# Letting four attention units lead, with gate products between their blocks, in a one-layer hybrid attention kernel

## The chip, the cores and the metric

The kernel runs on one core of a Trainium2 chip. A core has a matrix engine (TensorE: PE for its matmuls, PEld for loading their stationary operand), VectorE (DVE), ScalarE (ACT), GpSimd (POOL) and SyncE (SP), which here only issues DMAs. Each engine works through its own instructions in order; engines wait for each other by semaphores. SBUF is the memory beside the engines, PSUM the banks that matmuls write, DRAM lies behind the DMA queues. The metric is the device time of one execution in microseconds.

## The reference

One layer of a diffusion backbone: 1024 latent tokens and a prompt of 128 tokens, width 1024, all in float32. Each token is normed and modulated, projected once into queries, keys, values and gates of two mixers, attended in both, and the gated results are projected out and added to the residual.

```python
h = rmsnorm(xs, norm_gain) * (1.0 + scale) + shift
q_a, k_a, v_a, g_a, q_b, k_b, v_b, g_b = split(h @ w_in)      # q, k: RMS norm per head, axial rotary
o_a = global_attn_latent(q_a, k_a, v_a, cache_k_a, cache_v_a)       # 8 heads, 2 key heads: 128 cached + 1024 latent keys
o_b = window_attn_latent(q_b, k_b, v_b, cache_k_b, cache_v_b, sink) # |i - j| <= 128, cached keys, a sink logit
xs = xs + gate * (concat(o_a * silu(g_a), o_b * silu(g_b)) @ w_out)
```

The prompt goes through the same weights and attends to its own 128 keys. Its keys and values are outputs too.

## The kernel before

Tokens are nine tiles of 128 (tile 0 is the prompt, 1 to 8 the latents). For precision nearly every operand is held as a high part, rounded to the matmul's format, and a low part, the rest; a product is two or three matmuls (high x high, high x low, low x high). So most results are copied once by ACT (the high part) and subtracted once by DVE or POOL (the low part).

The order of the work is that of the Python program: `in_order` at its end (L94) ties every instruction to the one before it on its engine. `tick` (L131) advances a counter, `later(n, f)` (L127) puts a piece of work n ticks ahead. The stages:

1. Norm and modulation, gates of mixer A, then queries of A and of B, which go to DRAM (`q_dram`), then keys and values of both mixers (L749 to L838). Keys of A lie in `kha`, `kla` (high, low), of B in `khb`, `klb`; values in `v_hi`, `v_lo`, where `v_hi` has a half for each mixer.
2. Gates of mixer B, `gates(W_GB, ...)` (L301, L839, L1060): 12 pieces, four for each of the token ranges 0:512, 512:768 and 768:1152 (`THIRDS`). A piece is 24 matmuls, then `put_gates` (L286): one Silu on ACT and a store to DRAM. Between their products run the maxima of two A units (`EARLY`, L1047).
3. The main loop (L1262). A unit is one token tile, one mixer and one key head with its four query heads. Units go in the order A, B, A, B (L849), 32 of them, and the prompt's four last. An A unit has nine key blocks, a B unit three or four. Each pass of the loop is a slot and starts one block: `scores` (L1107), and three slots later (`LAG`) `values` (L1134).

In an A block PE makes two score matmuls of 512 columns, ACT the exponential (L1123) and the high part (L1127), POOL the low part (L1131; DVE for one block in nine), PE three value matmuls (L1141 to L1144). The exponential needs each query's maximum: `max_items` (L864) makes 12 matmuls of 384 columns with a DVE maximum each, some slots ahead. A B unit's `weight_items` (L910) make scores of four heads against `khb`, `klb`, a DVE maximum (L942) and an exponential; its blocks are then PE transposes (L1115).

When a unit's last values are done, `inverse`, `gated` and `parts` (L1150 to L1179) follow at 1, 4 and 6 slots: division, the product with the Silu gate, and the split into `ogh` and `ogl`. Nine slots after a B unit's last values, `out_items` (L1199) of this token tile's group (A's and B's parts) are queued: 24 matmuls of 512 columns with `w_out`. The loop takes 2.5 of them in a slot (`OUTRATE`), 3 in an empty one.

`w_out` is split into parts that take the memory of the modulated tokens as these are used up (`load_wo`, `split_wo`, `WO_STEPS`, `WO_LATE`). After the gates, `p1.close()` (L1067) gives the memory of the gate weights to later tiles, and an ACT table with Exp and Ln is loaded (L1069). Loads and most stores stand in SP's queue, in program order.

## Time and profile before

| | before |
|---|---|
| median of 3 runs | 711.63 us (710.87 to 712.46) |
| profiled execution, first to last instruction (span) | 709.6 us |
| median less span | 2.0 us |
| PE busy, share of the span | 691.6 us, 97% |
| DVE, ACT, POOL busy | 469.3, 409.9, 334.2 us |
| dense stages (projections and gates) | from about 17 to 303 us |
| main loop, first score product to last output product | 303.2 to 704.9 us |
| one steady pair of units (A and B) | 23.88 us |
| DRAM read, written | 58.7 MB, 19.2 MB |

The page of a profile gives, in this order: busy time of each engine; the span in 40 slices, a digit for the busy tenths of each; DMA queues; the chain of work that ended last; the costliest groups of instructions (line, engine, operation, output<-inputs, shapes, count | busy us, mean ns of one | idle time of the engine before them and what ended it); DMA issues. Matmuls overlap in the records: one lasts some 390 ns from start to end while the next starts some 230 ns after it. The profiled execution's own time is not given apart from its span; the three runs are other executions.

### The profile page before, as it was taken

Reading aid. Unit: us, or ns where it says so; the run is one execution under the profiler, and the core shown is the slowest. Engines: PE = TensorE matmul, PEld = TensorE weight load, DVE = VectorE, ACT = ScalarE, POOL = GpSimd, SP = SyncE. Lnnn points to the kernel's source line nnn. Section 1 sums busy time; section 2 is a strip of 40 time slices with the busy share of each in tenths; the row PEclk is TensorE's granted clock in tenths of the full one; section 3 lists DMA queues with packets and bytes.
Section 4 is the critical chain, followed back from the end, with each engine's and each line's share of the span. In section 5 each row is a group of like instructions: output and inputs, shape, how many; then the busy total and the mean of one; then the engine's idle time right before and its main releaser. Section 6 shows DMA issues by size and latency. Waiting matters only on the chain. (4 is left out here: it accounts for less than half of the span.)

```text
span 709.6 us, 10604 instructions
## 1 busy us (share of the span) xinstructions
PE 691.6 (97%) x3508; PEld 558.5 (79%) x3508; DVE 469.3 (66%) x1019; ACT 409.9 (58%) x829; POOL 334.2 (47%) x356
## 2 busy tenths in 40 slices
PE   7999999999999999989999999999999999999987
PEld 4778988878787889966788888888888888787865
DVE  4667257967848945647867578666775776675662
ACT  5646412412403431188777887787778777877760
POOL 3547023233213421256756655665576557555660
PEclk9999999999999999999999999999999999999999
DMA  8962283358353116332222121212221221222323
GB/s 316 415 211 102 78 302 74 90 154 263 84 139 104 37 39 215 123 108 57 78 68 85 50 82 53 71 57 75 68 82 38 79 71 50 78 72 70 104 67 121
DMA packets 53560, 78.58 MB, mean 111 GB/s; under 512 B 7096, under 2 KB 25720, under 8 KB 52608
## 3 DMA queue, kind: packets, MB, share of 16 engines
q1 hardware_dynamic: 45328, 65.96, 28.1%
q10 hardware_dynamic: 8176, 11.94, 6.3%
q8 instruction: 28, 0.46, 0.3%
q14 instruction: 28, 0.23, 0.1%
HBM read 58.69 MB, written 19.18 MB: 110 GB/s over the span
## 5 line engine op out<-in xcount | busy, mean ns | idle before, releaser
L1131 POOL TENSOR_TENSOR pl<-pe,ph 128x512 fp32r<-128x512 f32 x130 | 167.7, 1292 | 145.0 <-DVE nm L942 67.5
L882 DVE TENSOR_REDUCE mx<-pmx 128x1 f32<-128x384 f32 x192 | 101.4, 552 | 56.3 <-PE pmx L881 54.8
L1123 ACT ACTIVATE pe<-st 128x512 f32<-128x512 f32 x146 | 86.8, 594 | 28.2 <-PE st L1121 27.4
L1127 ACT CAST ph<-pe 128x512 fp32r<-128x512 f32 x146 | 90.6, 621 | 4.8
L1141 PE MATMUL pv<-ph,v_hi 128*128 128x512 f32 x208 | 82.8, 398 | 2.2 <-DVE spare L1165 2.2
L1144 PE MATMUL pv<-pl,v_hi 128*128 128x512 f32 x208 | 82.4, 396 | 0.0
L1212 PE MATMUL po<-wo,ogh 128*128 128x512 f32 x216 | 72.6, 395 | 0.2 <-DVE yt L1219 0.2
L174 POOL TENSOR_TENSOR rs_q<-ms_q,mhalf 128x8 f32<-128x8 f32 x18 | 34.1, 1896 | 80.9 <-DVE ms_q L172 80.9
L942 DVE CUSTOM_DVE_ANT_0 sn<-sn,mask,nsink 128x512 f32<-128x512 f32 (+1 forms) x64 | 46.4, 724 | 38.0 <-PE sn L939 37.6
L881 PE MATMUL pmx<-kha,qt 128*128 128x384 f32 x192 | 61.2, 363 | 0.4 <-ACT pen L928 0.2
L1120 PE MATMUL st<-qt,kha 128*128 128x512 f32 x144 | 58.2, 404 | 1.9 <-ACT pe L1123 1.1
L1121 PE MATMUL st<-qb,kla 68*128 68x512 f32 x144 | 57.5, 399 | 1.1 <-DVE qb L901 1.1
L1143 PE MATMUL pv<-ph,v_lo 128*64 128x512 f32 x146 | 57.6, 395 | 0.0
L1144 PEld LDWEIGHTS pv<-pl,v_hi 128*128 128x128 f32 x208 | 39.2, 189 | 16.4
L928 ACT ACTIVATE pen<-sn,nm 128x512 f32<-128x512 f32 (+2 forms) x72 | 45.0, 626 | 6.5 <-DVE nm L942 3.1
L1116 ACT CAST ph<-st 128x512 fp32r<-128x512 f32 x62 | 36.4, 587 | 19.9 <-PE st L1115 18.7
L1141 PEld LDWEIGHTS pv<-ph,v_hi 128*128 128x128 f32 x208 | 39.3, 189 | 10.6 <-ACT ogh L1177 2.4
L646 ACT CAST qo0q<-ptq 128x512 fp32r<-128x512 f32 x18 | 10.6, 586 | 60.7 <-PE ptq L643 55.8
L1212 PEld LDWEIGHTS po<-wo,ogh 128*128 128x128 f32 x216 | 40.0, 188 | 6.8 <-DVE yt L1219 0.6
L1117 DVE TENSOR_TENSOR pl<-st,ph 128x512 fp32r<-128x512 f32 x62 | 42.5, 686 | 2.7 <-ACT ph L1116 2.1
L1212 PE MATMUL po<-wo,ogl 128*128 128x512 f32 x108 | 42.6, 394 | 0.0
L881 PEld LDWEIGHTS pmx<-kha,qt 128*128 128x128 f32 x192 | 35.6, 191 | 6.4 <-DVE mx L882 1.3
(213 smaller groups left out, 1699.2 us busy)
## 6 DMA issues: line engine op xcount, KB each, us to landing
qt<-qd SPq DMA_DIRECT2D x36, 256.0 KB, 3.0
wm<-in_w_mod_ss_dram SPq DMA_DIRECT2D x7, 1024.0 KB, 10.0
qd<-qo0q ACTq DMA_DIRECT2D x36, 128.0 KB, 2.4
qd<-qo1q ACTq DMA_DIRECT2D x36, 128.0 KB, 2.4
sgl<-gd SPq DMA_DIRECT2D x36, 128.0 KB, 2.2
out_dram<-yt SPq DMA_DIRECT2D x17, 256.0 KB, 2.0
xn<-in_x_sample_dram SPq DMA_DIRECT2D x8, 512.0 KB, 7.2
wg<-in_w_mod_g_dram SPq DMA_DIRECT2D x4, 1024.0 KB, 8.3
```

Of the source, the lines that this page charges most:

```text
L881: nc.tensor.matmul(pm[:, 0:384], lhs, kha[:, g, 3 * b : 3 * b + 3, :], start=True, stop=True)
L882: nc.vector.tensor_reduce(mx[:, h, b : b + 1], pm[:, 0:384], axis=AX.X, op=ALU.max)
L942: nc.vector.tensor_tensor_reduce(s, s, mask[:, m0 : m0 + n], -1.0, nsink[:, 4 * g + h : 4 * g + h + 1], op0=ALU.add, op1=ALU.min, accum_ou ...
L1120: nc.tensor.matmul(s, kh, qtile[i], start=True, stop=False)
L1121: nc.tensor.matmul(s, kl, qbtile[i], start=False, stop=True)
L1123: nc.scalar.activation(pe, s, AF.Exp)
L1127: nc.scalar.copy(ph, pe)
L1131: nc.gpsimd.tensor_tensor(pl, pe, ph, op=ALU.subtract)
L1141: nc.tensor.matmul(pv, two, ph, start=(b == 0), stop=False)
L1143: nc.tensor.matmul(pv[0:64, :], vl, ph, start=False, stop=False)
L1144: nc.tensor.matmul(pv, two, pl, start=False, stop=last)
L1212: nc.tensor.matmul(po[n], a, wo_parts[KT * n + k][lo], start=(k == KS[0] and p == 0), stop=(k == KS[-1] and p == 2))
```

## The change

- Only the first four pieces of mixer B's gates (tokens 0:512) are made in the dense stage, with the maxima of the first A unit beside the last two. The other eight pieces, 192 matmuls, become a list `light` of single products: 12 units of them (a unit is a product of 512 columns) before the first slot, then 4.2 in each slot (`fill`).
- Their Silu can't be had from the ACT table that the main loop uses. `late_gates` makes it of a DVE maximum, Exp, Ln (of 1 + x), Exp on ACT, and `late_put` of a DVE product, then the store.
- The unit order is A0 A1 A2 A3, then A4 B0 A5 B1 ... A15 B11, then B12 to B15, each behind five empty slots (`GAP`), then the prompt's four. In the tail the output products go at 4 a slot (`OUTTAIL`), and the B units' small steps are closer (`EX_TAIL`, `ROWS_TAIL`).
- An A unit's gated output waits in DRAM (`of_dram`) until its B unit starts: `fetch` loads it there, and three slots later `split_out` makes `ogh` and `ogl`.
- The low parts of B's keys and both parts of B's values go to DRAM as they are made (`klb_dram`, `vb_dram`), and come back in one load each when the gate pieces are done and `p1` is closed (`finished`, three slots after the last product).
- The last parts of `w_out` are loaded and split in other slots (`WO_MID`, `WO_LAST`).

The core of the diff ("..." marks lines left out):

```diff
+LEADERS = 4
+LIGHT = 4.2
+PRE = 6
+GAP = 5
+MX_LEADER = (0, 0, 1, 1, 2, 2, 3, 3, 4, 4, 5, 5)
+LEADER_END = 6
-WO_LATE = {12: 8, 13: 9, 11: 21, 14: 22, 15: 23}
+WO_MID = ((7, 4, 10), (8, 5), (9, 6), (10, 8))
+WO_LAST = ((12, 10, 11), (13, 11, 14), (11, 19, 15), (14, 20), (15, 24))
+EX_TAIL = (1, 1, 3)
+ROWS_TAIL = (1, 1, 3, 4)
+OUTTAIL = 4.0
...
-        gb = gates(W_GB, 1, None, THIRDS)
+        gb = gates(W_GB, 1, None, THIRDS[:1])
...
-    units = [(t, m, g) for t in range(1, NT) for g in range(2) for m in range(2)]
-    units[PROMPT_AT:PROMPT_AT] = [(0, m, g) for g in range(2) for m in range(2)]
+        order = [(t, 0, g) for t in range(1, NT) for g in range(2)]
+        units = order[:LEADERS]
+        for u, (t, m, g) in enumerate(order):
+            if LEADERS + u < len(order):
+                units.append(order[LEADERS + u])
+            units.append((t, 1, g))
+        units += [(0, m, g) for g in range(2) for m in range(2)]
...
+                    lb = kt.tile([P, 2, P], F32R, tag="lb", name=f"lb{nm}")
...
-                            low.append((klb[:, g, 1::3, :], four, khb[:, g, 1::3, :]))
...
+                    low.append((lb, p4[:, 2:4], khb[:, :, at, :]))
+                    def put_low():
+                        for a in (1, 4, 7, 10) if blk == 0 else (at,):
+                            nc.sync.dma_start(klb_dram[:, :, a, :], lb.bitcast(F32))
+                    later(2, put_low)
...
+    def late_gates(pg, ch, ts):
+        n = ts.stop - ts.start
+        sg = wrp.tile([P, 512], F32, tag="raw", name=f"sg1_{ch}_{ts.start}")[:, 0:n]
+        nc.vector.tensor_scalar(sg, pg, -80.0, None, op0=ALU.max)
+        nc.scalar.activation(sg, sg, AF.Exp, scale=-1.0)
+        nc.scalar.activation(sg, sg, AF.Ln, bias=1.0)
+        nc.scalar.activation(sg, sg, AF.Exp, scale=-1.0)
+        later(1, lambda: late_put(pg, sg, ch, ts))
+    def late_put(pg, sg, ch, ts):
+        nc.vector.tensor_tensor(sg, pg, sg, op=ALU.mult)
+        r0 = 512 + P * ch
+        nc.sync.dma_start(g_dram[r0 : r0 + P, ts], sg)
+    for a, b in THIRDS[1:]:
+        for ch in range(4):
+            light += piece_items(ch, slice(a, b), (lambda a=a: marks[a]()) if ch == 3 else None)
...
+    def finished(gate):
+        p1.close()
...
+        nc.sync.dma_start(klb.bitcast(F32), klb_dram)
+        nc.sync.dma_start(vb.bitcast(F32), vb_dram)
...
+        for i in (12, 13):
+            load_wo(i, late_pools["b2"])
+        wo_steps(WO_LAST)
+        for n in range(2):
+            nc.sync.dma_start(gate[n], gate_row[0:1, 512 * n : 512 * n + 512].to_broadcast([P, 512]))
...
+            if m == 0 and t:
+                nc.sync.dma_start(of_dram[t, g], v["of"])
+            else:
+                split_out(t, 2 * m + g, v["of"])
...
+    def fetch(t, g):
+        ofl = areas["spare"][:, 1280:1536].rearrange("p (c n) -> p c n", c=2)
+        nc.sync.dma_start(ofl, of_dram[t, g])
+        later(3, lambda: split_out(t, g, ofl))
...
+        if i >= TAIL and units[i][0]:
+            slots += [None] * GAP
...
+    def fill(n):
+        rate[0] = min(rate[0] + n, 8.0)
+        while light and rate[0] >= light[0][0]:
+            n, f = light.pop(0)
+            rate[0] -= n
+            f()
+    for _ in range(2):
+        fill(PRE)
+        tick()
...
-        for f in due.get(s, ()):
+        for f in due.get(s, ())[:1]:
             f()
-        rate = OUTRATE if s < len(slots) and slots[s] else PADRATE
-        credit = min(credit + rate, 6.0) if outq else 0.0
+        fill(LIGHT / 2)
+        for f in due.get(s, ())[1:]:
+            f()
+        fill(LIGHT / 2)
+        rate_ = OUTTAIL if s >= start[TAIL] - GAP else OUTRATE if s < len(slots) and slots[s] else PADRATE
+        credit = min(credit + rate_, 6.0) if outq else 0.0
```

More of the change, by code (lines that the diff above doesn't have):

```diff
@@ L33 @@
 WRAW = 3
-PROMPT_AT = 32
 KS = (0, 1, 4, 5, 2, 3, 6, 7)
@@ L1044, in hybrid_step @@
     later(2, lambda: nc.vector.tensor_copy(mask, mask32))
[L1045 to L1054 removed]
+    u_load(2)
     for i in range(4):
         load_wo(i)
[L1058 to L1059 removed]
@@ L1088, in blocks @@
         p0, p1_ = window(t)
         at = {p: b + 1 for b, p in enumerate(POS)}
-        return [(p - p0, v_hi[:, 1, 2 * at.get(p, 0) + g], None) for p in range(p0, p1_)]
+        return [(p - p0, 2 * at.get(p, 0) + g) for p in range(p0, p1_)]
     pvb, og = {}, {}
```

349 lines of the change are left out of this document (195 added, 154 removed).

## The prediction

> **What bounds the kernel now.** I read the page's busy table and slices first, then the busy time of each engine stage by stage, then the waits inside the stages that are not full. The page:
>
> ```profile
> span 709.6 us, 10604 instructions
> PE 691.6 (97%) x3508; PEld 558.5 (79%) x3508; DVE 469.3 (66%) x1019; ACT 409.9 (58%) x829; POOL 334.2 (47%) x356
> ACT  5646412412403431188777887787778777877760
> PEclk9999999999999999999999999999999999999999
> ```
>
> TensorE (PE) is the bound, at full clock, and the change neither adds nor removes a matmul. So the time can change only by the idle time of PE that it closes or opens, and by the pace of products that get other neighbours. The stages (columns: length, then busy us with the count of instructions for PE, weight load, DVE, ACT, POOL, then clock and DMA). The first two rows are the gate products of mixer B (dense stage); the next four and the last two are cut where a unit of mixer A begins its first scores:
>
> ```profile
> 272.00:284.00 12.00, 12.00 (x98) 12.00 (x97) 9.87 (x20) 1.15 (x3) 2.58 (x2) 1.00 0.65 200
> 284.20:303.10 18.90, 18.90 (x111) 18.74 (x110) 13.07 (x28) 1.86 (x4) 3.88 (x3) 1.00 0.37 122
> 303.18:321.90 18.72, 15.86 (x74) 10.90 (x72) 8.74 (x20) 16.83 (x35) 10.45 (x10) 1.00 0.34 98
> 321.90:341.64 19.74, 18.94 (x87) 13.93 (x88) 14.21 (x34) 16.28 (x35) 15.19 (x16) 1.00 0.26 78
> 341.64:367.12 25.48, 24.84 (x120) 19.77 (x119) 18.66 (x38) 19.67 (x39) 16.56 (x17) 1.00 0.26 77
> 390.96:414.84 23.88, 23.88 (x116) 19.24 (x116) 15.26 (x34) 18.73 (x38) 14.10 (x15) 1.00 0.21 64
> 650.53:673.66 23.13, 22.64 (x115) 18.21 (x114) 14.07 (x28) 18.67 (x44) 14.17 (x16) 1.00 0.36 118
> 673.66:704.88 31.22, 29.25 (x132) 22.43 (x130) 14.53 (x35) 13.15 (x32) 12.35 (x18) 1.00 0.29 90
> ```
>
> The reader is to see three regimes. In the dense stage PE is full and ACT nearly asleep (1.86 of 18.90 us). In the first two pairs of units (one of A, one of B) ACT is the full engine (16.83 of 18.72) and PE has holes, because no output products exist yet to fill them. From 391 us on every pair takes 23.88 us with PE full and ACT at 78%. The tail has small holes again. What fills ACT, POOL and DVE in a pair, from the page's costliest groups:
>
> ```profile
> L1131 POOL TENSOR_TENSOR pl<-pe,ph 128x512 fp32r<-128x512 f32 x130 | 167.7, 1292 | 145.0 <-DVE nm L942 67.5
> L882 DVE TENSOR_REDUCE mx<-pmx 128x1 f32<-128x384 f32 x192 | 101.4, 552 | 56.3 <-PE pmx L881 54.8
> L1123 ACT ACTIVATE pe<-st 128x512 f32<-128x512 f32 x146 | 86.8, 594 | 28.2 <-PE st L1121 27.4
> L1127 ACT CAST ph<-pe 128x512 fp32r<-128x512 f32 x146 | 90.6, 621 | 4.8
> L942 DVE CUSTOM_DVE_ANT_0 sn<-sn,mask,nsink 128x512 f32<-128x512 f32 (+1 forms) x64 | 46.4, 724 | 38.0 <-PE sn L939 37.6
> L1117 DVE TENSOR_TENSOR pl<-st,ph 128x512 fp32r<-128x512 f32 x62 | 42.5, 686 | 2.7 <-ACT ph L1116 2.1
> ```
>
> and smaller ones from the groups by line (all of the kernel, the gate stage, the second pair, a steady pair):
>
> ```profile
> L1156 ACT ACTIVATE rs<-rs 64x512 f32<-64x512 f32 x18 | 11.4, 632 | 0.6
> L1155 ACT ACTIVATE rs<-pv 64x512 f32<-64x512 f32 x18 | 10.7, 594 | 13.0 <-PE pv L1144 11.9 <-DVE spare L1165 1.0
> L290 ACT ACTIVATE sg<-pg 128x384 f32<-128x384 f32 x4 | 2.0, 492 | 17.1 <-PE pg L259 12.8 <-PE ptm L900 4.2
> L290 ACT ACTIVATE sg<-pg 128x256 f32<-128x256 f32 x4 | 1.5, 384 | 11.8 <-PE pg L259 11.8
> L1177 ACT CAST ogh<-spare 128x256 fp32r<-128x256 f32 x2 | 0.8, 399 | 0.0
> L1165 DVE TENSOR_TENSOR spare<-pv,rs 64x256 f32<-64x256 f32 x4 | 1.7, 413 | 0.0
> L942 DVE DVE_READ_ACCUMULATOR2_ANT nm<- 128x1 f32 x4 | 0.5, 127 | 0.0
> ```
>
> **Prices of PE.** The end of the chain of waits prices an output product, and the two DVE sums of each half row:
>
> ```profile
> 688.03 5.48 PE po L1212 x24
> ...
> 693.54 0.71 DVE po L1218
> ...
> 694.27 0.70 DVE yt L1219
> ...
> 695.01 9.85 PE po L1212 x42
> ```
>
> (5.48 + 9.85) / 66 = 0.232 us, which I use for any product of 512 columns. A steady pair without its 24 output products takes 23.88 - 24 x 0.232 = 18.31 us for 92 matmuls, 0.199 each.
>
> **Term 1, the start that is removed.** 74 matmuls at 0.199 are 14.73 us, so the first pair idles 3.99; 87 are 17.31, the second idles 2.43; the third holds the 92 and 28 output products, 18.31 + 6.50 = 24.81, and idles 0.67. Together 7.1 us. In the new order A0 starts with gate products beside it and this idle goes: -7.1. The Trainium skill, Perfetto Trace Analysis, section "Identifying the Most-Contended Engine", says that busy matmuls are a poor gauge and the busy share of the weight loads a better one. By it, with 19.24 / 23.88 = 0.806 as full, the three pairs idle 5.2, 2.5 and 0.9, 8.6 us in all, and the whole forecast would be 1.5 us lower; the trace agrees with it on where the holes are.
>
> **Where the hole reappears.** I count slots of the main loop (one block each). There are 8 moved pieces of 24 products: four of 256 columns and four of 384, together 48 + 72 = 120 units of a 512-column product. 12 go before slot 0 and 4.2 in each slot, so they end in slot 25. The four leaders fill slots 0 to 35, A4 36 to 44, B0 45 to 47, A5 48 to 56. Output products come 12 slots after the last block of a B unit: slot 59 for B0 (slot 23 before). So slots 26 to 58 have neither gate nor output products. They are the old first 23 slots over again, ten slots of A alone longer.
>
> **Term 2, start of the loop.** A0's second score matmul waits for its row of maxima, as this one did:
>
> ```profile
> 651.47 0.50 PE L1121 MATMUL st<-qb,kla 68*128 68x512 f32 x1 [0.49 <-DVE qb L901]
> ```
>
> +0.5 (0 to 0.9, if the gate products before it cover it or DVE is late with the weight splits).
>
> **Term 3, pace of the moved products.** Dense they took 12.00 / 98 = 0.122 and 18.90 / 111 = 0.170 us. Among others nothing shows them; the nearest bounds are no change and 0.01 more each (192 x 0.01 = 1.9). I take the middle, +1.0. In their slots PE needs 5 x 0.232 + 4.2 x 0.232 + 12/9 x 0.18 = 2.4 us (a product of the maxima is one of 384 columns), ACT 0.594 + 0.621, POOL 1.292, and DVE, which in the second pair has 14.21 us in 12 slots with maxima and weight splits, 1.2. The three ACT instructions that replace each Silu (8 x 2 more at 0.384 or 0.492, 7.0 us in all, and two DVE ones each) are covered by PE and cost nothing; without that cover they would cost those 7.
>
> **Term 4, ten slots of A alone (26 to 35).** PE: 50 x 0.232 + 17 maxima x 0.18 = 14.7 us. ACT: 10 x 1.215, the inverse of one unit (0.594 + 0.632) and the last gate piece (3 x 0.492): 14.9. Two full engines: idle like the third pair (3%, 0.4) to like the second (12%, 1.8): +1.0.
>
> **Term 5, B's operands from DRAM.** klb (1.5 MB) and v_b (1.25 MB) are asked for on SP after slot 28, when the gate stage's memory is free, followed by two w_out tiles, two gate rows and, at slot 31, B0's queries (1.25 MB more). PE needs klb and the queries at slot 36: if late, PE, in order, stops with A4's scores behind it. The cover is 8 x 1.49 = 11.9 us. The nearest row is a pair of 1 MB loads:
>
> ```profile
> wg<-in_w_mod_g_dram SPq DMA_DIRECT2D x4, 1024.0 KB, 8.3
> DMA to landing us min/median/max: 8.2/8.3/8.5
> ```
>
> Both land after 8.3 us, so about 2 MB in 8.3. If klb must wait for all 4 MB, that is 16 us and a stall of 4; if for its own share, none. I take +0.5 (0 to 4). The Trainium skill, DMA: Bandwidth & Descriptors, gives 2 us plus bytes over 436 GB/s ("Anatomy of one DMA") and says that descriptors of a ring are consumed in order ("Queues, rings and completion order"). By it klb, issued first, would take 5.6 us and this term would be 0. The trace does not bear it out: the first wg load would then have taken 4.4, not 8.2.
>
> The small transfers (A's outputs out and back, 128 KB each, 22 stores of keys and values) cost nothing: a fetch has three slots of 23.88 / 13 = 1.84 us before its use, and a store on SP waits for POOL's product of two slots earlier, with the next gate and query loads behind it that are due slots later. Uncovered, each fetch would cost its landing, about that of a load of the same size:
>
> ```profile
> sgl<-gd SPq DMA_DIRECT2D x36, 128.0 KB, 2.2
> ```
>
> **Term 6, pairs A4+B0, A5+B1, A6+B2.** The first two have the old second pair's work without its 0.8 us of output copies on ACT; w_out splits load DVE as before. Between 0.67 and 2.43 I take 1.6 each, and 0.67 for the third: +3.9 (2.0 to 5.5).
>
> **Steady pairs.** Same instructions beside each other, so 23.88 us; no term.
>
> **Term 7, the tail.** B12 to B15 now run without an A unit: five empty slots and 4 (or 3) blocks each, output products at 4 a slot, 24 for each unit. Thus 6 of 9 slots have them and 3 do not; around B12 it is 6 slots in a row (195 to 200). There PE has four blocks' transposes (four small ones each, at half the mean price of 0.199: 0.4), three blocks' values (2 x 0.232) and two heads' scores (2 x 0.232), 3.9 us; DVE 4 x 0.686 + 2 x (0.724 + 0.127) + 2 x 0.413 = 5.3: 1.4 idle. At B14 and B15, with three such slots each, I count half, 0.7. Against these, the wait quoted in term 2 and those of the prompt's units go in part, as more output products stand between:
>
> ```profile
> 683.53 0.47 PE L1141 MATMUL pv<-ph,v_hi 128*128 128x512 f32 x1 [0.94 <-DVE spare L1165]
> 687.32 0.47 PE L1141 MATMUL pv<-ph,v_hi 128*128 128x512 f32 x1 [0.69 <-DVE spare L1165]
> ```
>
> That is -1.7 of 0.49 + 0.94 + 0.69 = 2.1. Sum 1.4 + 0.7 + 0.7 - 1.7 = +1.1; bounds -1.7 (nothing lost) and 4 x 1.4 = +5.6. What follows the last product stays.
>
> **Term 8, keys and values.** DVE saves two of these minus one subtraction of half the size, about 0.9 us:
>
> ```profile
> 235.31 1.27 DVE L763 TENSOR_TENSOR klb<-ptc,khb 128x512 fp32r<-128x512 f32 x2
> 228.72 0.52 PE L745 MATMUL ptk<-ident_r,k2k 128*128 128x128 f32 x3 [1.25 <-DVE klp L763]
> ```
>
> PE waits for DVE there only once, earlier; and the new stores, waiting for DVE, stand before the loads of the gate weights on SP. 0 (-0.9 to +1).
>
> **Sum:** -7.1 + 0.5 + 1.0 + 1.0 + 0.5 + 3.9 + 1.1 + 0 = +0.9, from 709.6 to 710.5 us of span. The median of the runs, 711.63, is 2.0 above the span, so 712.5.
>
> **Rivals.** *Faster: the second hole stays shut.* If ACT, without output copies, keeps ahead in slots 26 to 58, terms 3 to 6 shrink to 0.3, 0.4, 0 and 2.0, and the tail gains 1.7: -7.1 + 0.5 + 2.7 - 1.7 = -5.6, 706. For it: ACT's 16.28 us in the second pair are less than PE's 17.31. Against: that pair still took 19.74. *Slower: the tail of lone B units.* Each B's chain (scores, DVE, exponentials, transposes, subtraction) ends after its neighbour's output products have run out, 1.4 us four times and nothing recovered: terms 1 to 6 are -0.2, so +5.4, 717. It decides when PE idles over 3.5 us in slots 190 to 223. Against it: over its nine slots a lone unit has 24 x 0.232 + 16 x 0.232 + 4 x 0.4 = 10.9 us for PE, and 4 x 0.851 + 4 x 0.686 + 0.83 + 2 x 1.41 = 9.8 for DVE. *Slower: operands late,* 4 us instead of 0.5 in term 5: 716. *The change doesn't fill what it means to:* ACT, in order, waits for each finished gate piece and starves the scores beside it, 0.4 us for each of 8 pieces: 715.5. Against: 0.5 us and more of slack per slot.
>
> **Numbers.** Forecast 0.44 (own range 709 to 716), faster rival 0.33, tail 0.13, late operands 0.06, starved scores 0.04. What a measurement can tell from no change is 0.2%, 1.4 us. Of the forecast's 0.44, 0.07 lie below 710.2, 0.21 within, 0.16 above 713.1. Faster 0.33 + 0.07 = 0.40; same 0.21; slower 0.16 + 0.23 = 0.39. The low bounds of all terms add to -7.3 (704.3); the range ends there, at 704, and above just past the tail rival, 718.
>
> **What would show it.** Right: PE full from the first dense product to slot 25 at about 2.4 us a slot; ACT near full and PE with holes of 5 us in all between there and the first output product; the steady pair at 23.9; holes of some 3 us in the lone B units. Wrong: no holes after the gate products end (then 706); a single PE wait of microseconds on the load of klb or of B0's queries; a pair that is no longer 23.9 us, which no term holds.

## The result, and the profile after

The changed kernel takes **735.17 us** (median of 4 runs, 733.63 to 735.69); the kernel before, on the same chip, 711.40 (710.87 to 712.46). The ratio is 1.033, 95% interval 1.0315 to 1.0344: slower by 23.8 us. The forecast was 712.5, range 704 to 718. The profiled execution took 734.87 us, 2.07 above its span, as before (2.0); so 23.2 us lie between the two spans. Its page, and the clock of its core:

```profile
span 732.8 us, 10800 instructions
PE 700.3 (96%) x3508; PEld 561.4 (77%) x3508; DVE 482.7 (66%) x1034; ACT 419.4 (57%) x855; POOL 338.6 (46%) x356
```

```profile
core 0: 732.8 us, clock 0.992
```

The number of matmuls is unchanged (3508), yet PE's busy time rose by 8.7 us: busy is not work. The clock says part of why: 0.992 here, 0.999 in the profile before. The same stages as in the prediction, cut where the first gate product of mixer B starts, where A0, A1, A4, A5 and A6 begin their first scores, at slot 26, and around one steady pair and the tail (columns as there: length, busy us and count for PE, weight load, DVE, ACT, POOL, then clock and DMA):

```profile
249.91:278.39 28.48, 28.48 (x148) 24.36 (x147) 16.93 (x44) 7.91 (x19) 4.64 (x4) 1.00 0.33 109
278.39:304.78 26.39, 22.10 (x126) 18.80 (x124) 23.20 (x36) 13.33 (x26) 12.27 (x10) 0.94 0.36 121
304.78:344.80 40.02, 40.02 (x203) 35.35 (x202) 24.55 (x48) 28.28 (x51) 25.44 (x20) 1.00 0.24 77
344.80:363.86 19.06, 16.71 (x74) 12.11 (x72) 13.17 (x26) 14.43 (x26) 12.18 (x10) 1.00 0.72 267
363.86:383.98 20.12, 19.13 (x89) 13.89 (x88) 13.67 (x33) 16.64 (x35) 15.04 (x15) 1.00 0.26 80
383.98:407.45 23.47, 20.64 (x89) 15.31 (x88) 17.16 (x36) 17.75 (x37) 16.31 (x17) 0.93 0.23 69
...
456.57:480.53 23.96, 23.96 (x116) 19.10 (x116) 15.19 (x34) 19.36 (x39) 14.14 (x16) 1.00 0.26 82
645.20:694.44 49.24, 43.00 (x223) 33.62 (x222) 31.45 (x72) 25.68 (x71) 12.51 (x24) 1.00 0.39 115
694.44:727.95 33.51, 30.69 (x139) 23.83 (x138) 15.12 (x36) 12.70 (x34) 12.42 (x18) 1.00 0.27 91
```

The reader is to see four things. The first unit (278 to 305) is long and DVE is the fullest engine in it, 23.20 of 26.39 us, at a clock of 0.94. The middle of the gate products (305 to 345) is as meant, PE full. The three stretches after that have holes again, the last of them with a clock of 0.93. The lone units of B (645 to 694) have PE idle for 6.2 us by busy time alone. A steady pair is still 23.9 us.

To put all of it on one scale I use a line, 0.0194 us a matmul and 0.0428 us per 100 columns, which leaves next to nothing in a steady pair. It gives 0.239 us for a product of 512 columns and 0.184 for one of 384, near the prediction's 0.232 and 0.18. Summed over the matmuls of a stage that is its need; what a stage lasts beyond it is called idle here and holds rests, slow clock and small losses alike (negative where products run faster than the line).

| stage | before, us | after, us | difference | by the prediction |
|---|---|---|---|---|
| keys and values, up to the first gate product of B | 1.1 | 3.5 | +2.3 | 0 (term 8) |
| dense gate products (all, or the first third and 12 more units) | -2.5 | -0.7 | +1.9 | +1.0 (term 3) |
| A0's first scores to the end of the third pair (before 303 to 367, after 278 to 433) | 8.0 | 17.1 | +9.1 | -1.2 (terms 1, 2, 4, 5, 6) |
| one steady pair | 0.1 | 0.1 | 0 | 0 |
| tail, first scores of the last A unit to the last output product (before 651 to 705, after 623 to 728) | 4.3 | 13.7 | +9.4 | +1.1 (term 7) |

The 17.1 divide into 4.3 (slots 0 to 25), 3.4 (26 to 35), 2.5 (A4 and B0), 6.1 (A5 and B1) and 0.7 (A6 and B2). The split depends somewhat on the prices: with 0.232, 0.18, 0.122 and 0.1 us for 512, 384, 256 and 128 columns, the prediction's own, the dense row is +1.0, the start +11.3 and the tail +8.7. (The expectations below, written with a slightly different line, have 13.9 for the tail, 3.2 for slots 26 to 35.)

**What a rest costs.** PE in the start of the loop, with the waits in brackets:

```profile
283.02 0.45 PE L899 MATMUL pmx<-kha,qt 128*128 128x384 f32 x1 [1.44 <-DVE mx L900]
...
284.43 0.39 PE L1205 MATMUL st<-qt,kha 128*128 128x512 f32 x1
284.65 0.40 PE L1206 MATMUL st<-qb,kla 68*128 68x512 f32 x1
287.08 0.44 PE L899 MATMUL pmx<-kha,qt 128*128 128x384 f32 x1 [2.03 <-DVE mx L900]
...
288.87 0.63 PE L1205 MATMUL st<-qt,kha 128*128 128x512 f32 x1
289.30 0.63 PE L1206 MATMUL st<-qb,kla 68*128 68x512 f32 x1
```

The two score products stand 0.22 us apart at 284.4 and 0.43 apart at 288.9, after a rest of 2.03 us. The same happens behind the rests at 229.7 and 386.4 (2.0 and 1.9 us). The stretches of doubled spacing, with the granted clock in the last column but two:

```profile
230.20:233.60 3.40, 3.40 (x11) 2.62 (x10) 3.33 (x12) 1.26 (x5) 0.67 (x1) 0.50 0.14 48
288.20:291.60 3.40, 3.40 (x15) 3.21 (x14) 3.34 (x6) 0.03 (x1) 2.45 (x2) 0.51 0.37 105
387.20:390.60 3.40, 3.40 (x11) 2.72 (x10) 1.37 (x4) 3.09 (x7) 2.31 (x3) 0.50 0.31 98
```

Each is 3.4 us at half speed and so costs 1.7 us; the three cost 5.1. The kernel before has none from 13 us to its last product. What DVE did around the rest at 287:

```profile
283.35 1.54 DVE L1116 CAST wo<-wraw 128x512 fp32r<-128x512 f32 x1
284.92 1.64 DVE L1117 TENSOR_TENSOR wo<-wraw,wo 128x512 fp32r<-128x512 f32 x1
286.48 1.01 DVE L900 TENSOR_REDUCE mx<-pmx 128x1 f32<-128x384 f32 x2
287.42 0.41 DVE L1116 CAST wo<-wraw 128x512 fp32r<-128x512 f32 x1
```

A cast of a w_out tile takes 0.41 us at 287.4 and 1.54 at 283.3; its subtraction 1.64. GpSimd's subtractions of low parts run beside the long ones:

```profile
283.31 2.70 POOL L1213 TENSOR_TENSOR pl<-pe,ph 128x512 fp32r<-128x512 f32 x2 [26.62 <-DMA wraw<-in_w_out_dram]
```

The maxima, for which PE waits, stand behind the splits. Seven casts and four subtractions take 10.7 of DVE's 23.2 us in this unit; at 0.417 and 0.693 us, as in the kernel before where GpSimd is idle (275.6 and 276.1 us), they would take 5.7. In the kernel before 11 of the 16 casts and 6 of DVE's 8 subtractions are done ahead of the loop; here all come behind A0's first scores.

### The profile page after: what moved, and what is told of

Read it like the earlier page. It is cut to its first block, busy times and chain, and to the rows that moved or that the text cites. A ratio compares the mean times of both kernels' runs of the same rounds, so it can differ in the third digit from the quotient of the medians.

```text
span 732.8 us, 10800 instructions
## 1 busy us (share of the span) xinstructions
PE 700.3 (96%) x3508; PEld 561.4 (77%) x3508; DVE 482.7 (66%) x1034; ACT 419.4 (57%) x855; POOL 338.6 (46%) x356
## 4 chain that ended last, share of the span: by engine, by line
PE 81%; DVE 9%; ACT 3%; issue 3%; DMA 3%; POOL 1%; ACTq 0%; SPq 0%; DVEq 0%; POOLq 0%
PE po L1308 13%; PE pv L1223 6%; PE pv L1226 6%; PE pq L256 5%; PE pq L254 5%; PE pmx L899 4%; PE pq L255 4%; PE st L1205 4%; PE st L1206 4%; PE pv L1225 4%; PE st L1200 3%; PE pg L960 3%; PE sn L1018 2%; PE sn L1019 2%; PE pg L264 2%
## 5 line engine op out<-in xcount | busy, mean ns | idle before, releaser
L899 PE MATMUL pmx<-kha,qt 128*128 128x384 f32 x192 | 63.1, 365 | 6.2 <-DVE mx L900 5.7
L1223 PE MATMUL pv<-ph,v_hi 128*128 128x512 f32 x146 | 57.9, 396 | 0.3 <-DVE spare L1251 0.3
L1226 PE MATMUL pv<-pl,v_hi 128*128 128x512 f32 x146 | 57.5, 394 | 0.0
L899 PEld LDWEIGHTS pmx<-kha,qt 128*128 128x128 f32 x192 | 36.0, 191 | 15.9 <-DVE mx L900 10.3
L652 ACT CAST qo0q<-ptq 128x512 fp32r<-128x512 f32 x18 | 10.6, 586 | 60.6 <-PE ptq L649 55.8
L1200 PE MATMUL st<-ident_r,pen 128*128 128x128 f32 x248 | 37.3, 273 | 2.6 <-DVE pl L1202 2.6
L1276 POOL TENSOR_TENSOR ogl<-spare,ogh 128x256 fp32r<-128x256 f32 x36 | 26.3, 737 | 28.9 <-ACT ogh L1274 24.7
```

The source lines that it names most:

```text
L899: nc.tensor.matmul(pm[:, 0:384], lhs, kha[:, g, 3 * b : 3 * b + 3, :], start=True, stop=True)
L1200: nc.tensor.transpose(s[:, P * h : P * h + P], penat[i][:, h, o : o + P], ident_r.bitcast(F32))
L1223: nc.tensor.matmul(pv, two, ph, start=(b == 0), stop=False)
L1226: nc.tensor.matmul(pv, two, pl, start=False, stop=last)
```

## The experiments

All times are medians of 4 runs, ratios are to the kernel before on the same chip (its medians there are 711.4 to 712.3).

| kernel | us | ratio, 95% |
|---|---|---|
| the change | 735.17 | 1.0330 (1.0315 to 1.0344) |
| tail spread | 731.55 | 1.0274 (1.0251 to 1.0298) |
| tail rows later | 734.05 | 1.0305 (1.0285 to 1.0326) |
| tail, two sets | 731.90 | 1.0275 (1.0253 to 1.0298) |
| w_out split by ScalarE | 733.14 | 1.0280 (1.0252 to 1.0309) |
| gate product later | 734.97 | 1.0315 (1.0267 to 1.0364) |
| maxima in other banks | 735.61 | 1.0327 (1.0299 to 1.0355) |
| 2 of 9 copies on DVE | 740.86 | 1.0402 (1.0380 to 1.0424) |
| 4 of 9 copies on DVE | 747.10 | 1.0501 (1.0456 to 1.0546) |
| low part on GpSimd | 737.28 | 1.0342 (1.0311 to 1.0373) |
| buffers of keys and values | 735.97 | 1.0333 (1.0312 to 1.0353) |
| keys' sum on GpSimd | 736.09 | 1.0330 (1.0303 to 1.0358) |
| dense gates, 4 leaders | 744.93 | 1.0460 (1.0432 to 1.0487) |
| dense gates, 2 leaders | 737.83 | 1.0359 (1.0324 to 1.0393) |
| dense gates, 1 leader | 740.14 | 1.0396 (1.0372 to 1.0419) |
| three mends | 729.10 | 1.0238 (1.0203 to 1.0273) |
| mends and two sets | 729.59 | 1.0229 (1.0191 to 1.0267) |
| the same, one empty slot | 727.34 | 1.0214 (1.0194 to 1.0234) |
| all mends | 728.60 | 1.0224 (1.0189 to 1.0259) |

### The tail

**Output products spread over the whole unit.**

```diff
-OUTTAIL = 4.0
+OUTTAIL = 2.7
```

> One constant: in the tail the output products go out at 2.7 a slot instead of 4, so the 24 of a unit last nine slots instead of six. Theory A (the prediction's: TensorE idles in those slots of a lone B unit that have no output products): the idle of the tail, 13.9 us in the changed kernel (645 us to the end of the last product), falls to about 7, the time by 6 to 8 us, from 735.2 to about 728. Theory B (the chain of a lone B unit, DVE and GpSimd with their waits, sets the pace, whatever stands between): the time stays within 1.5 us.

Measured 731.55, 3.6 us less. The waits of PE in the tail of the changed kernel (what was waited for, us, times, longest), and the last output products in its chain of waits:

```profile
PE sn L1018 <- ACT pen L1008: 2.9, 3, 1.4
PE st L1200 <- DVE pl L1202: 2.6, 3, 1.4
PE pv L1223 <- DVE spare L1251: 2.5, 1, 2.5
```

```profile
717.84 10.08 PE po L1308 x42
```

and of the kernel with the spread products:

```profile
PE pv L1223 <- DVE spare L1251: 1.3, 1, 1.3
PE sn L1018 <- ACT pen L1008: 1.2, 2, 0.8
```

```profile
714.00 10.08 PE po L1308 x42
```

The last 42 products begin 3.84 us earlier, of which 0.75 came from ahead of the tail (the last unit of A begins its scores at 622.93 and 622.18). So theory A holds in direction and at half its size: the idle of the tail falls from 13.7 to 10.6, not to 7.

**The row of inverse sums fetched and used later.**

```diff
-ROWS_TAIL = (1, 1, 3, 4)
+ROWS_TAIL = (1, 1, 4, 6)
```

> One tuple: in the tail the row of inverse sums is fetched from DRAM one slot later and GpSimd multiplies it into the gate two slots later (the distances of the rest of the kernel). Theory C (GpSimd, in order, stands 18.1 us in five waits for this row in the tail and holds back the sums of the next unit): the waits shrink below 5 us and the time falls by 3 to 5 us, to about 731. Theories A and B of the tail (products run out, or DVE's chain): the same within 1 us, since GpSimd is not what TensorE waits for.

Measured 734.05. One wait of PE shrinks: values before DVE's product into the output, from 2.54 us to 1.46. PE's other waits in the tail are the same to 0.1 us. GpSimd's waits for the row fell from 18.1 to 13.3 us, not below 5. Theory C named a real wait, worth 1 us, not 3 to 5: PE stands behind GpSimd in one place only.

**Two sets of exponentials.** The unit's four rows go to idle tiles in every second lone unit, and the scores begin five slots ahead of the unit, beside the blocks of the one before.

```diff
-GAP = 5
+GAP = 2
-                penat[i] = late_pools["qp2"].tile([P, 4, 512], F32, tag="pen", name=f"pen{i}")[:, :, 0:n]
+                if i >= TAIL and (i - TAIL) % 2 == 0:
+                    penat[i] = [w3.tile([P, 512], F32, tag="pe", ...)[:, 0:n] for h in range(3)]
+                    penat[i].append(late_pools["qp2"].tile([P, 512], F32R, tag="qt", ...).bitcast(F32)[:, 0:n])
+                else:
+                    ...
```

> The lone units of B write their exponentials alternately into two sets of tiles (three tiles of A's exponentials and one of the queries stand idle there), so that the scores of a unit run beside the blocks of the one ahead; in return two empty slots stand before a lone unit instead of five. Theory L (a lone unit is a chain in a row, scores, DVE, exponentials, transposes, since it has one set of exponentials, and TensorE idles in it): the tail's idle falls from 13.9 to about 7 and the time by 5 to 8 us, to 727 to 730. Rival M (DVE's work for a lone unit, worked out at 9.8 us, sets the pace however it is laid out): within 1.5 us of 735.

Measured 731.90. From the first scores of the last A unit to the last output product the profile has 103.5 us against 105.0, and an idle of 12.2 instead of 13.7. But 1.7 of the 12.2 are a half-speed stretch from 696.4 us, and the changed kernel's profile has none in its tail. Without it 10.5 are left: theory L holds in direction, at less than half its size, and M falls (DVE is busy 45 of 81 us). The waits are now two of DVE's product into the output (3.3 us) and one of 1.8 on ScalarE's exponentials. So the tail is a chain of small dependences, part of which reappears at another link. The lowest idle that a kernel with four lone units reached is 10.1 us (all mends, below), 1.7 of it slow clock; what the remaining 8.4 hang on was not taken apart further.

### The start of the loop and the slots without output products

**w_out split by ScalarE and GpSimd.**

```diff
-        nc.vector.tensor_copy(hi, raw)
-        (nc.gpsimd if i % 2 else nc.vector).tensor_tensor(lo, raw, hi, op=ALU.subtract)
+        nc.scalar.copy(hi, raw)
+        nc.gpsimd.tensor_tensor(lo, raw, hi, op=ALU.subtract)
```

> The 16 tiles of w_out are split by ScalarE (high part) and GpSimd (low part), none by DVE. Theory D (in the first slots and at A5+B1 TensorE stalls since DVE does the splits, stretched beside GpSimd, ahead of maxima and of the queries' row): the stalls of 1.61 and 2.22 us at 283 and 287 us and the one of 2.18 at 386 us go, with the low clock behind them, and the time falls by 4 to 8 us, to 727 to 731. Rival E (DVE is late there because its gate product waits for the three ScalarE steps before it): the first two stalls stay, ScalarE gets 16 copies of about 0.6 us more, and the time is within 2 us of 735, or above.

Measured 733.14. Its A0, and A4 with B0, cut as the rows of the changed kernel:

```profile
277.09:299.15 22.06, 20.07 (x125) 17.45 (x124) 13.29 (x25) 17.96 (x35) 17.11 (x14) 1.00 0.45 146
...
358.24:380.92 22.68, 19.33 (x90) 13.84 (x88) 11.84 (x29) 18.18 (x38) 15.94 (x16) 1.00 0.24 77
```

The first unit takes 22.06 us instead of 26.39, with the clock at 1.00; the idle of slots 0 to 25 goes from 4.3 to 0.2, 1.7 of it by the clock; the rest of 1.9 us at A5 is 0.5. Theory D holds for these. But A4 with B0 grew from 20.12 to 22.68. The waits of PE in this stretch, first of the changed kernel, then of this one:

```profile
PE pmx L899 <- DVE mx L900: 5.7, 6, 2.0
PE st L1206 <- DVE qb L918: 2.4, 2, 1.9
```

```profile
PE pmx L899 <- DVE mx L900: 3.3, 4, 1.5
PE st L1206 <- DMA qb<-qd: 2.3, 2, 1.7
```

A new one stands there: 1.7 us for a DMA, A4's queries (tile `qb`), asked for behind klb and v_b. SP's issues in the changed kernel, and the product that uses the queries:

```profile
350.18 0.40 SPq L1154 DMA_DIRECT2D klb<-klbd  x1
...
353.88 0.45 SPq L904 DMA_DIRECT2D qb<-qd  x1
...
364.38 0.47 PE L1206 MATMUL st<-qb,kla 68*128 68x512 f32 x1
```

and in the kernel with the splits moved:

```profile
344.55 0.40 SPq L1154 DMA_DIRECT2D klb<-klbd  x1
...
348.86 0.45 SPq L904 DMA_DIRECT2D qb<-qd  x1
...
360.34 0.47 PE L1206 MATMUL st<-qb,kla 68*128 68x512 f32 x1 [1.70 <-DMA qb<-qd]
```

From the issue of klb to the product that uses the queries are 14.2 us in the first kernel and 15.8 in the second. In both, A4's first score product (363.86 and 358.24 us) begins 13.7 us after klb's issue, since that issue moves with the slots. So PE did not come earlier to the loads here: they landed 1.6 us later. 0.6 of it is the issue of the queries itself (4.3 us behind klb's instead of 3.7); the rest is open. The profiled execution, which has no half-speed stretch, is 4.8 us shorter than that of the changed kernel, as theory D has it. The other three, at clocks of 0.990 to 0.992, are only 1.0 to 1.7 us shorter than it, and the median is 2.0 below the change's.

**DVE's product of a gate piece one slot later.**

```diff
-        later(1, lambda: late_put(pg, sg, ch, ts))
+        later(2, lambda: late_put(pg, sg, ch, ts))
-        later(3, lambda: finished(gate))
+        later(4, lambda: finished(gate))
```

> DVE's product of a moved gate piece is issued one slot later (and with it the end of the gate stage's memory). Theory E (DVE, in order, waits 1.38 us at 280.7 us for the three ScalarE steps, and the maxima behind it stop TensorE): the stall of 1.61 us at 283 us goes, like smaller ones at the seven other pieces: 1.5 to 3 us less, about 733. Theory D (the splits of w_out do it): within 1 us of 735.

Measured 734.97. The rest at 283 us goes and the one at 287 grows to 4.0 us. DVE's wait for ScalarE was not the cost: the rest only moved to the next split. D, not E.

**The maxima in other banks.**

```diff
-                pm = bank("A", f"pmx{i}_{h}_{b}")
+                pm = bank("DE"[(3 * h + b) % 2] if i in (4, 6, 8) else "A", f"pmx{i}_{h}_{b}")
```

> The maxima of A4's, A5's and A6's units (computed between the end of the gate products and the first output product) go to the two PSUM banks that stand empty in these slots, instead of to the two that B's scores and the transposes share. Theory N (TensorE waits there for a bank: product of the maxima behind DVE's maximum or ScalarE's exponential): the idle between 344 and 406 us falls from 12 to about 7, the time by 4 to 6 us, to about 730. Theory O (ScalarE, 82 to 94% busy there, sets the pace; term 4 of the prediction): within 1.5 us of 735.

Measured 735.61: N falls. The idle from slot 26 to the first output product is 12.5 us; it was 11.9 without the edit.

**Copies from ScalarE to DVE, two and four of nine blocks in units A3 to A6.**

```diff
-        nc.scalar.copy(ph, pe)
+        (nc.vector.tensor_copy if i in (3, 4, 6, 8) and b in (2, 6) else nc.scalar.copy)(ph, pe)
```

(four: b in (0, 2, 6, 8).)

> In units A3 to A6 DVE makes the rounded copy of the exponentials for two of the nine blocks instead of ScalarE (0.62 us each there). Theory O (ScalarE sets the pace of the slots without fillers): its work between 344 and 406 us falls by about 4 of 47.9 us, and the time by 2 to 4 us, to about 732. Theory Q (the chain of single waits between TensorE, DVE and ScalarE sets it, no engine being full: ScalarE 78%, DVE 70%, TensorE 90% busy): within 1.5 us of 735, or above, since DVE is then later with maxima.

> The same for four of the nine blocks. Theory O: another 2 to 4 us less (728 to 731) until DVE is as full as ScalarE. Theory Q: 735 or above.

Measured 740.86 and 747.10. The dose works the other way: 5.7 us for 8 copies, 11.9 for 16, about 0.7 a copy (in the profiles 1.7 and 5.1 us of the loss from slot 26 to the first output product are slow clock). So theory O, ScalarE as the pace (terms 4 and 6), falls. DVE in the four-block kernel, from 344 to 418 us (busy us, mean ns, idle before them and what ended it):

```profile
L900 DVE TENSOR_REDUCE mx<-pmx 128x1 f32<-128x384 f32 x41 | 21.3, 550 | 5.4 <-PE pmx L899 5.0
L1209 DVE CAST ph<-pe 128x512 fp32r<-128x512 f32 x12 | 7.1, 591 | 10.0 <-ACT pe L1208 10.0
```

A copy costs DVE 0.59 us and another 0.83 of standing in front of it for ScalarE's exponential, with the maxima queued behind. PE's waits for the maxima in this stretch are

```profile
PE pmx L899 <- DVE mx L900: 7.2, 5, 2.0
```

against 2.3 us in the changed kernel (345 to 406 us). What these slots wait for is DVE's order, not the sum of an engine's work.

**The fifth block's low part on GpSimd in the same units.**

```diff
-        if b in PL_DVE:
+        if b in PL_DVE and i not in (3, 4, 6, 8):
```

> In units A3 to A6 the low part of the fifth block's exponentials is GpSimd's like that of the other eight, not DVE's. Theory R (DVE, in order, waits in front of this instruction for ScalarE's copy, 5.3 us in three waits, and the maxima behind it stop TensorE): the stall of 1.70 us at 358 us goes, with its like at the neighbours, and the time falls by 1.5 to 3 us, to about 733. Rival (GpSimd, 71% busy there, is then late with its low parts): 735 or above.

Measured 737.28 at a profiled clock of 0.985 (0.992 in the change): no gain. The rest at 358 us, 1.70 counted from start to start (1.53 in the trace's bracket), went down to 0.65 (0.47), as theory R says, and A3 fell from 17.12 to 15.91 us. A4 with B0 rose from 20.12 to 21.63: A4 now comes 12.5 us after klb's issue instead of 13.7, and waits 1.78 us for its queries. So the stall is DVE's order, and taking it away in this place earns nothing while B's operands land when they do.

### Keys and values

**More buffers for the stores.**

```diff
-                    lb = kt.tile([P, 2, P], F32R, tag="lb", name=f"lb{nm}")
+                    lb = kt.tile([P, 2, P], F32R, tag="lb", name=f"lb{nm}", bufs=3)
-            vb = kt.tile([P, 2, 2, HD], F32R, tag="vb", name=f"vb{j}")
+            vb = kt.tile([P, 2, 2, HD], F32R, tag="vb", name=f"vb{j}", bufs=4)
```

> The tiles that carry B's values and the low parts of B's keys to DRAM have four and three buffers instead of two. Theory F (in the stage of keys and values ScalarE waits 6.8 us in three waits for the store of an older tile, and TensorE behind it 2.21 us at 229.7 us, after which the granted clock is 0.83 for 10 us): that wait and the low clock go, and the time falls by about 3.5 us (0.8 of wait beyond the 1.42 that the kernel before also had, 1.7 of clock, and up to 1 of shorter ones). Rival G (DVE's own work sets that wait, with ScalarE's wait beside it): the time stays within 1 us.

Measured 735.97. ScalarE's wait is gone, and PE's is not. The changed kernel, ScalarE's wait, PE's, and the ten us behind it:

```profile
ACT vb L785 <- DMA vbd<-vb: 6.8, 3, 3.1
```

```profile
229.71 0.41 PE L751 MATMUL ptk<-ident_r,k2k 128*128 128x128 f32 x2 [2.03 <-DVE klp L774]
```

```profile
230.00:240.00 10.00, 10.00 (x44) 8.11 (x42) 7.34 (x28) 3.88 (x13) 1.84 (x3) 0.83 0.65 197
```

and the kernel with more buffers:

```profile
229.66 0.41 PE L751 MATMUL ptk<-ident_r,k2k 128*128 128x128 f32 x2 [2.04 <-DVE klp L774]
```

```profile
230.00:240.00 10.00, 10.00 (x51) 8.29 (x50) 8.82 (x33) 3.88 (x13) 3.12 (x4) 1.00 0.63 190
```

Theory F falls: one of ScalarE's largest waits there cost nothing. And the same rest of 2.04 us was followed by a clock of 1.00 here and of 0.83 there, 51 matmuls in ten us against 44.

**The keys' sum on GpSimd.**

```diff
-                    nc.vector.tensor_tensor(k2, *(two(a) for a in v["rot"]), op=ALU.add)
+                    nc.gpsimd.tensor_tensor(k2, *(two(a) for a in v["rot"]), op=ALU.add)
```

> In the stage of keys and values the sum of the two rotary products of a sample tile (0.68 us of DVE) is GpSimd's. Theory P (DVE, 97% busy from 220 to 230 us, brings the low key parts late, and TensorE, which needs the bank, rests 2.21 us at 229.7): the rest falls below 1 us, the clock in the ten us after stays at 1.00, and the time falls by 2 to 3 us, to about 732.5. Rival (GpSimd's slower sum lengthens the chain of the tile itself): the wait stays, the time is 735 or more.

Measured 736.09. The rest falls from 2.03 to 1.42 us and comes 1.1 us earlier, so DVE was late as theory P has it; but GpSimd is then late with the low part of a gate weight, and PE waits 0.82 us for that at 251 us. The first gate product comes 2.3 us earlier, with no low clock ahead of it, and A0 0.7; yet the time stays. The profile has a half-speed stretch in the tail, 1.7 us, that the changed kernel's has not. Why DVE began this stage later than before isn't settled.

### Parts of the change

**All gate products dense**, with four, two and one leading unit (the first output of A then lies in the later area, which the last edit does; with one leader the load of the fourth unit's queries also no longer waits for an older unit's last use):

```diff
+    while light:
+        fill(PRE)
+        tick()
+    for _ in range(4):
+        tick()
-            if i < 2:
+            if False:
```

> The 192 moved gate products run densely before the first slot, as in the kernel before; leaders, tail and DRAM passages stay as changed. Theory H (the moved products do fill what they are meant to, at a price): the dense pace comes back, 1.9 us, and the stalls at 283 and 287 us go with 1.7 of clock, about 4; but slots 0 to 25 are then like slots 26 to 35, where 10 slots idled 3.2 us, so some 8 more: the time rises to about 737 (735 to 740). Rival I (putting these products among the blocks is itself what costs the time): it falls by 4 us or more, to 731 or below.

> As the dense kernel, with two leading units of A instead of four (so two lone units of B at the end). Theory J (the price goes with the number of leaders: slots before the first output product fall from 59 to 41, lone units of B from four to two): the tail's idle falls from 13.9 to about 9, the start's by a third, the time is 8 to 11 us below the dense kernel with four leaders. Rival K (the passages through DRAM and the moved loads cost it, whatever the order): within 3 us of that kernel.

> As the dense kernel, with one leading unit of A, so that the order is the one before but for one unit; A's outputs, B's values and low key parts still go through DRAM. Theory J: one lone unit is left in the tail and 32 slots before the first output product, so another 4 to 5 us less, within 5 us of the kernel before (711 to 717), plus what B's operands, loaded only some 10 slots before their use, cost if they are late. Rival K: 725 or more.

Measured 744.93, 737.83 and 740.14. Against theory I, the interleaving is worth 9.8 us: without it the slots from A0 to the third pair idle 21.8 us, and the dense stage doesn't get its pace back, since each piece now holds its bank through three ScalarE steps and a DVE product:

```profile
PE pg L960 <- DVE sg L980: 4.1, 3, 2.5
```

(the waits of PE from 250 to 310 us in the dense kernel). H was right in direction and 8 us short in size; the profile's half-speed stretches cost 10.2 us, 5.1 more than in the change. From four leaders to two the time falls by 7.1 us, a little less than J's 8 to 11: the tail's idle is 15.9, 11.5 and 7.8 us with four, two and one, some 2.7 for each lone unit beyond the first. With one leader the time doesn't fall further: the next queries, asked for behind B's operands, stop PE:

```profile
PE pmx L899 <- DMA qt<-qd: 7.0, 1, 7.0
```

(waits of PE from 309 to 405 us in that kernel.) So J and K each hold a part. With only one leader the kernel is still 28 us above the one before, 10.2 of them slow clock in the profile: the order alone is not what costs.

### Mends together

Three mends: the spread products, the splits off DVE, and v_b asked for later.

```diff
-        nc.sync.dma_start(vb.bitcast(F32), vb_dram)
+        later(5, lambda: nc.sync.dma_start(vb.bitcast(F32), vb_dram))
```

> Three edits at once: output products at 2.7 a slot in the tail, w_out split by ScalarE and GpSimd, and the load of B's values five slots after that of the low key parts (in the run with the split alone, the queries of A4 or A5 stood 1.88 us behind these two loads). If the stalls are what they were named for, the gains add: 3.6 of the tail, 2 to 4.8 of the split, 1.9 of the load, and the time is 725 to 728. If the stalls only move (the sum of ScalarE's and DVE's work between 278 and 406 us is the limit), 729 to 732.

Measured 729.10, the near end of the second expectation (the executions lie at 727 and at 731): the wait for A4's queries stayed at 1.16 us (1.70 without the later load). With the two sets in place of the spread products, and two or one empty slots:

> The two sets of exponentials in the tail, with w_out split by ScalarE and GpSimd and the later load of B's values. By theory L and the run of the three mends (729.1), whose slower output products (3.6 us) this one replaces by a gain of 5 to 8: 724 to 728. If L falls: about 732.

> As the kernel with the two sets and the two other mends, with one empty slot before a lone unit instead of two. If slots without work of their own still cost time there: 1 to 2 us less. If TensorE or DVE is full in the tail by then: the same within 1 us.

Measured 729.59 and 727.34: the first between its two expectations, and the empty slot worth 2.3 us. And with the other banks and the keys' sum added:

> All mends in one: w_out split by ScalarE and GpSimd, the later load of B's values, two sets of exponentials with one empty slot before a lone unit (together 727.3), the maxima in other banks and the keys' sum on GpSimd. If N and P hold their gains add: 4 to 6 and 2 to 3 us less, 718 to 722; still above the kernel before. If only one holds: 722 to 726.

Measured 728.60: the last two add nothing, as they did alone. The best of them is 15.5 us above the kernel before; no version here beats it.

## Why the prediction was wrong

**Right.** The idle of the old start (term 1, 7.1 us; 8.0 by the line above); the steady pair; that the moved products fill the slots from A1 on (305 to 345 us, PE full); that the last gate piece ends at slot 25; the first output product at slot 59 (406 us). The dense runs confirm that the moved products must have cover: the price of three ScalarE steps without it was put at 7 us and 4.1 were measured.

**Term 7, the tail, failed by 8.3 us** (+1.1 against +9.4). The step that failed is the price of a lone unit: the work of DVE less that of PE in the slots without output products, 5.3 - 3.9 = 1.4, as if the fuller engine set the pace. The "I count half" for B14 and B15 and the deduction of 1.7 made it smaller still; PE's waits in the tail grew from 2.5 to 8.7 us. The run with the products spread gives the slots without output products 3 us. The rest is, by PE's waits, the lone unit's own chain, scores, DVE, exponentials, transposes, subtraction, in which PE waits for DVE and ScalarE by turns, though neither is full (31.45 and 25.68 of 49.24 us). The second set of exponentials, which shortens this chain, brings it down by 3.2 us beside the clock; for what is left no run names the link. The tail rival had this mechanism and the right threshold, and its price, 1.4 four times, was 3.8 us too small.

**Terms 2 and 3 and the start of the loop.** The 1.2 us that I gave DVE of a slot's 2.4 were a mean over 12 slots of the second pair. In the first nine slots DVE has two maxima in each of six, w_out splits, two steps for each gate piece, and no slack: 23.20 of 26.39 us. That 1.2 is the step that failed here: it has no term for the splits that the change moves from the dense stage into these slots. What the runs showed in its place: splits stretched beside GpSimd to 10.7 us, with the maxima behind them; with the splits off DVE the unit takes 22.06. That the added gate instructions cost nothing, as term 3 says, was not refuted: DVE's product one slot later left the time as it was.

**Terms 4 and 6** were worked out from ScalarE as the full engine. The two doses of copies show that giving ScalarE less and DVE more makes it worse at 0.7 us a copy. DVE's order is what these slots wait for. The worst pair, A5 with B1 (6.1 us idle for the 1.6 predicted, 1.7 of them slow clock), has two w_out steps at slots 47 and 48 in front of the queries' row; the chain of waits of the changed kernel:

```profile
384.30 0.59 DVE wo_big L1116
384.92 0.69 DVE wo_big L1117
385.64 0.69 DVE qb L918
386.38 0.50 PE st L1206
```

"w_out splits load DVE as before" was the step: over the kernel they take 19.2 us of it instead of 14.6, and they stand in another place of its queue.

**Term 5, B's operands: the size of the wait was right by luck.** PE waits 0.3 us at most. But the loads took long: A4's queries, behind klb, were there 14.2 us after klb's issue in the changed kernel and 14.5 to 15.9 in the others that waited for them, near the upper bound of 16. The cover put at 11.9 us was 13.7, since the slots ahead of A4 were slower than term 4 has them; that slowness hid the loads. Where these slots are faster (12.5 us) PE waits 1.78; where the loads land later, as with the splits moved, 1.70. It is a second limit beside the first, so mending the slots alone earned nothing. The formula that the prediction quotes for klb is given by the Trainium skill, DMA: Bandwidth & Descriptors, section "Anatomy of one DMA", for DMAs issued by GpSimd; these loads are SyncE's.

**Term 8** was put at 0 and measured 2.3: a rest longer by 0.8 us (2.03 against 1.25), and 1.7 of slow clock behind it. The saved DVE work did not help; the cause of the later start is open.

**The clock, a term that the prediction didn't have.** It took PE "at full clock" from the profile before. The three half-speed stretches of the changed kernel's profile cost 5.1 us of the 23.2, one each in the rows of keys and values, of A0 and of A5 with B1 (0.992 against 0.999, times 733 us, is the same 5). They come and go between executions. The three mends ran 725.1 and 725.6 us at 0.996 and 0.997, and 729.0 and 729.1 at 0.991 and 0.992. But four executions of the change itself show no such order (731.7 to 733.7 us at 0.992 to 0.995), and the kernel before had 0.994 to 1.000 on the chips of the experiments, 0.997 in the mean; so of the difference between the medians the clock is rather 3 us than 5, an estimate. I had this effect in no bound, but without it the kernel would still lie above the range's 718.

One sum of the prediction is off by a little: 8 pieces at 0.4 us on top of 712.5 give 715.7, not 715.5.

## What to carry to other kernels

Cost a moved step by what stands behind it in its engine's queue at the new place, in the busiest slots and not in a mean over a pair: an engine at 70% can be what all wait for when it works in order. Where a stall goes, ask which load was hidden by it; two limits that end within half a microsecond of one another must be mended together. And a kernel that keeps the matrix engine full has its clock as a hidden asset: each rest of two microseconds that a change opens may be paid nearly twice.

## What the runs showed of the hardware

**Rests of 2 us can cost the clock.** In the changed kernel rests of 2.03, 2.03 and 1.92 us (229.7, 287.1 and 386.4 us) were each followed by 3.4 us at half speed, a loss of 1.7; a rest of 2.54 at 705.6 was not. With more buffers the same rest of 2.04 us at 229.7 was not either. The starts of the three stretches are 58.0 and 99.0 us apart, 17 and 29 times 3.41, so they lie on a grid, and whether a rest of this length costs clock seems to hang on where it falls in it. The Trainium skill, TensorE: Matmul & The Clock Gate, section "What's actually happening", has the clock halved after an idle window of about 3.4 us, and says that the window runs free, so that its phase differs between runs. The halving agrees with products 0.43 us apart instead of 0.22, and the free phase with the grid and the dips that come and go. The length of the idle time doesn't: here rests of about 2 us, with small ones around them, were enough.

**DVE beside GpSimd.** The same cast took 0.41 and 1.54 us, the same subtraction 0.69 (at 384.9 us) and 1.64. The short ones named here have no GpSimd instruction beside them, the long ones do. Not every one beside GpSimd is stretched: a cast at 322.1 us took 0.41 with GpSimd busy throughout. The difference, 0.95 to 1.13, is less than one of GpSimd's subtractions (1.3 us in the prediction's groups). The Trainium skill, SBUF — State Buffer, section "SBUF: two separate sides", says that DVE and GpSimd take one pair of ports in turn, for a whole instruction each, when DVE reads two operands from there or copies in its fast form; DVE's maxima, read from PSUM, took 0.55 us each everywhere, which agrees. The runs show the stretch; that it is the ports was not tested apart.
